# RWKV preparation in a hybrid layer: systems stored before the bonus, merged blocks evicted by ACT, new priorities

## The chip, the cores and the metric

The kernel runs on one core of a Trainium2 chip. The metric is the device time of one execution in microseconds. The core has a tensor engine (TensorE; PE in the profile, PEld for its weight loads), DVE, ACT and POOL for element-wise work, and SP, which here issues all DMAs. TensorE writes to banks of PSUM, from which DVE or ACT must copy ("evict") the results; everything else lies in SBUF, and large tensors in HBM.

## The reference, cut to what matters

One layer over 2048 tokens of width 1024. The input is modulated and projected; the projection feeds three groups of heads: (A) spatial gating, (B) RWKV-7 time mixing, (C) attention over a band of chunks. Each is gated, and one output projection with a residual and a layer norm follows. The change is in group B:

```python
def step(state, inp):
    r_t, w_t, k_t, v_t, a_t, b_t = inp
    sa = jnp.einsum('bhvk,bhk->bhv', state, a_t)
    state = state * w_t[:, :, None, :] + sa[..., None] * b_t[:, :, None, :] + v_t[..., None] * k_t[:, :, None, :]
    return state, jnp.einsum('bhvk,bhk->bhv', state, r_t)
...
y = layer_norm(y, ...)
y = y + jnp.sum(rh * kh * r_k, axis=-1, keepdims=True) * vh
```

The last line is the *bonus*: a term per token that does not need the state.

## The kernel before, in words

The tokens are cut into four stretches `u` of 512; RWKV has three pairs of heads `p`, so there are 12 RWKV *units* (p, u), counted here from 0 in the order in which they run. Within a unit there are 8 chunks of 64 tokens (`C`, `NC8`). Inside a chunk the recurrence is written as a triangular system, so that the state moves only once per chunk. A unit passes through these steps, each a Python generator:

- `rwkv_prep`: products with the small decay matrices (PE rows `rwp<-lo,lora`), scan and exponentials, then for each half of the chunks (four chunks, `c0`) the products of all keys with all queries (the Gram products, PE rows `rwp<-lr,bk` and `at<-lr,bk`). DVE evicts them with a mask: one diagonal half goes to `gb` (the systems), the other is written into `lr`. POOL scales the systems in `gb` by `rnc`. Then the 32 x 32 blocks of the systems are transposed on DVE (`gt`, in the buffers named `rc`), stored to HBM by four DMAs (`nd`), loaded back in another layout by four more (`ns`, one buffer only), and `ti` is loaded with the start of the solution. Last come the scaling of `bk` by `pend` on POOL and the bonus: `kp`, its high and low part, two products with `ones_r`, and `bon`, of which there are two buffers.
- `rwkv_solve`: 31 steps of forward substitution on DVE, two instructions each (`pr<-ti,ns` and `ti<-pr`). The solution goes to HBM (`td`) and back as `tt`. Two small groups of 16 products (PE rows `rwp<-pr,gb` and `rwp<-tt,pr`) merge the 32 x 32 blocks into 64 x 64 ones; the result of each is evicted into SBUF by two copies (`xx`, in the buffer named `pr`, and `tt`).
- `rwkv_late`: transposes and values that the chain needs.
- `rwkv_chain`: for each chunk three dependent products on TensorE with ACT and DVE work between them (PE rows `rc<-sv,lr`, `rc<-rhs,tt`, `rc<-sav,bt`), and after every fourth chunk the outputs (`rc<-sv,lr` of 64 columns and `rc<-sad,gb`). The chains of the 12 units follow each other, since the state is carried.
- `rwkv_post`: norm, four transposes (PE rows `rwp<-kc,pg`), bonus and gate, store of `y`; it frees the unit's gate buffer (`gateb`, two of them) and its `bon`.

Beside these run other generators: the projections (PE rows `pj<-hh,wh`, `pj<-hl,wh`, `pj<-hh,wl`: groups of 24 products of 512 columns; products into a tile `pj` are counted below as "projections", from the kernel's first one on), attention units (PE rows `sc`, `at<-kc,pexp`, `at<-pT,vt`), gating units (`at<-kc,tmp`), and at the end the output projection (also `pj`).

The order of all instructions is set while the kernel is built. A planner (`Model`, `drive`) keeps a clock for every engine, steps through the generators, lets a generator go on when what it yields is ready by that clock, and orders the instructions of each engine by readiness and priority. `until(key)` holds a generator back until a key is in `done`. `PREP` and `SOLVE` give each unit a priority for its preparation and for its solve. The engines then run the orders exactly as written.

In `rwkv_prep` before, everything from the transpose on waits for `("solved", previous unit)`; the unit is announced (`sent`) at the very end, after the bonus; `prepare` begins a unit when `("post", the unit two before)` is done.

Of the kernel before, what the change touches and what calls it, by code (L numbers as in the profile page):

```python
# [11 lines left out]
ALU = mybir.AluOpType  # L12
# [8 lines left out]
C = 64  # L21
NOSYNC = mybir.DependencyInfo(mybir.DependencyClass.NoSync, mybir.DependencyReason.DATA)
NC8 = U // C
# [254 lines left out]
def kernel(  # L278
# [7 lines left out]
    PE, V, A, G, SP = (Engine(md, e, n) for e, n in ((nc.tensor, "PE"), (nc.vector, "DVE"), (nc.scalar, "ACT"), (nc.gpsimd, "POOL"), (nc.sync, "SP")))  # L286
# [68 lines left out]
    mask = kc[:, K_MASK:K_MASK + 128]  # L355
# [76 lines left out]
    done = set()  # L432
# [12 lines left out]
    def until(*keys):  # L445
        while not all(k in done for k in keys):
            yield None
# [131 lines left out]
    HS = [slice(0, 64), slice(64, 128)]  # L579
    OS = [slice(64, 128), slice(0, 64)]  # L580
    c3 = lambda ap: ap.rearrange("p (c t) -> p c t", t=C)


    def rwkv_prep(p, u, before):
        yield from need(("lo", u), ("k", p, u), ("r", p, u), ("v", p, u))
        lo, k, r, v = (got[n] for n in (("lo", u), ("k", p, u), ("r", p, u), ("v", p, u)))
        b = P_PAIR + p * N_PAIR
# [18 lines left out]
        pend = sb([128, NC8], "pend", bufs=2)  # L606
# [7 lines left out]
        bk = sb([128, NC8, 2, C], "bk")  # L614
        lr = sb([128, NC8, 2, 2, C], "lr", bufs=2)
# [8 lines left out]
        for h in range(2):  # L624
            q = HS[h]
# [3 lines left out]
        for h in range(2):  # L629
            q = HS[h]  # L630
# [13 lines left out]
        rnc = sb([128, NC8], "rnc", bufs=2)  # L644
# [5 lines left out]
        gb = sb([128, NC8, 2, C], "gb", bufs=2)  # L650
        for c0 in range(0, NC8, 4):
            yield R(bk, lr, banks=("rwp", "at"))
            pg = rwp(), at()
            for c in range(4):
                for h in range(2):
                    q = HS[h]
                    mm(pg[h][:, c * 128:(c + 1) * 128].rearrange("p (s t) -> p s t", s=2), bk[q, c0 + c].rearrange("p s t -> p (s t)"),
                       lr[q, c0 + c, :, h, :])
            for h in range(2):
                for q, o in ((HS[h], gb[HS[h], c0:c0 + 4]), (OS[h], lr[OS[h], c0:c0 + 4, :, h, :])):  # L660
                    V.tensor_tensor(o, pg[h][q].rearrange("p (c s t) -> p c s t", c=4, s=2),
                                    mask[q].rearrange("p (s t) -> p s t", s=2).unsqueeze(1).to_broadcast([64, 4, 2, C]), ALU.mult)

        G.tensor_tensor(gb[:, :, 0, :], gb[:, :, 0, :], rnc.unsqueeze(2).to_broadcast([128, NC8, C]), ALU.mult)
        if before:
            yield from until(("solved",) + before)

        nd = dr([4, NC8, 32, 32], "nd", 2)
        td = dr([32, 32, 32], "td", 2)
        gt = sb([128, NC8, C], "rc", bufs=2)  # L670
        V.transpose(gt, gb[:, :, 0, :])
        for q in range(4):
            SP.dma_start(nd[q].rearrange("c t s -> t c s"), gt[32 * q:32 * q + 32, :, 32 * (q % 2):32 * (q % 2) + 32])
        ns = sb([128, 32, 32], "ns")
        for j in range(4):
            SP.dma_start(ns[32 * j:32 * j + 32].rearrange("p t s -> p (t s)"), nd.rearrange("q c t s -> (q c) (t s)"))
        V.memset(ns.rearrange("p t s -> p (t s)")[:, 0:1024:33], 1.0)
        ti = sb([128, 8, 32], "ti")
        SP.dma_start(ti.rearrange("p j i -> p (j i)"), cst[:, K_T0:K_T0 + 256])


        G.tensor_tensor(bk.rearrange("p c s t -> p c (s t)"), bk.rearrange("p c s t -> p c (s t)"),
# [8 lines left out]
        pbn = rwp()  # L691
        mm(pbn, ones_r, rkh, True, False)
        mm(pbn, ones_r, rkl, False, True)
        bon = sb([128, U], "bon", bufs=2)
        V.tensor_tensor(bon, pbn, v, ALU.mult)

        if p == 2:
            free(("lo", u))
        free(("r", p, u), ("k", p, u))
        unit[p, u] = dict(p=p, u=u, bk=bk, lr=lr, gb=gb, v=v, bon=bon, pend=pend, rnc=rnc, ns=ns, ti=ti, td=td)  # L700
        done.add(("sent", p, u))


    def rwkv_solve(s):
        p, u, gb, ns, ti, td = (s[n] for n in ("p", "u", "gb", "ns", "ti", "td"))
        yield R(ns, ti)
        pr = sb([128, 8 * 32], "pr")
        for i in range(1, 32):
            prv = pr[:, 0:8 * (i + 1)].rearrange("p (j s) -> p j s", j=8)
            V.tensor_tensor(prv, ti[:, :, 0:i + 1],  # L710
                            ns[:, i, 0:i + 1].unsqueeze(1).to_broadcast([128, 8, i + 1]), ALU.mult)
            V.tensor_reduce(ti[:, :, i], prv, AX.X, ALU.add)
            if i % 2:
                yield R(ti)
        for j in range(4):
            SP.dma_start(td.rearrange("y j i -> y (j i)")[:, j * 256:(j + 1) * 256],
                         ti[32 * j:32 * j + 32].rearrange("p j i -> p (j i)"))
        tt = tts[uorder.index((p, u)) % 2]
        for q in range(4):
            o = 32 * (q % 2)  # L720
            SP.dma_start(tt[32 * q:32 * q + 32, :, q // 2, o:o + 32],
                         td[8 * q:8 * q + 8].rearrange("c j i -> j c i"))
        tn = sb([128, NC8, 32], "pr")
        for h in range(2):
            q = slice(64 * h, 64 * h + 32)
            V.transpose(tn[q], tt[q, :, h, 0:32])
        yield R(tn, banks=("rwp",))
        px = rwp()
        for c in range(NC8):
            for h in range(2):  # L730
                a, z = 64 * h, 64 * h + 32
                mm(px[z:z + 32, c * 32:(c + 1) * 32], gb[a:a + 32, c, 0, 32:64], tn[a:a + 32, c, :])
        xx = sb([128, NC8, 32], "pr")
        for h in range(2):
            z = 64 * h + 32
            V.tensor_copy(xx[z:z + 32], px[z:z + 32, 0:256].rearrange("p (c t) -> p c t", t=32))
        yield R(xx, banks=("rwp",))
        px = rwp()
        for c in range(NC8):
            for h in range(2):  # L740
                a, z = 64 * h, 64 * h + 32
                mm(px[a:a + 32, c * 32:(c + 1) * 32], xx[z:z + 32, c, :], tt[z:z + 32, c, h, 32:64])
        for h in range(2):
            a = 64 * h
            V.tensor_copy(tt[a:a + 32, :, h, 32:64], px[a:a + 32, 0:256].rearrange("p (c t) -> p c t", t=32))
        s["tt"] = tt


# [276 lines left out]
    unit = {}  # L1025
# [246 lines left out]
    ORDER = [z.split() for z in ("B0 C0 G0 C1 B1 A0 G1 B2 C2 G2 A1", "A1 B0 C0 G0 C1 B1 G1 C2 B2 G2 A0",  # L1272
                                 "A0 C0 B0 G0 B1 C1 C2 B2 G1 G2 A1", "A1 B0 G0 B1 C0 A0 G1 B2 C1 G2 C2")]

    PREP = [4, 4, 4, 4.5, 2, 4, 4, 4, 6.5, 6.5, 5.5, 4]
    SOLVE = [4.5, 4, 3, 2, 4, 4, 6.5, 4, 3, 2, 2, 5.5]
    pprio, sprio = [4], [4]
    uorder = [(int(w[1]), u) for u in range(NU) for w in ORDER[u] if w[0] == "B"]

# [26 lines left out]
    def prepare():  # L1306
        yield from until("tables")
        for n, (p, u) in enumerate(uorder):
            if n > 1:
                yield from until(("post",) + uorder[n - 2])  # L1310
            pprio[0] = md.prio = PREP[n]
            yield from rwkv_prep(p, u, uorder[n - 1] if n else None)
            if n:
                yield from until(("chain",) + uorder[n - 1])
            yield from rwkv_late(unit[p, u])
            done.add(("late", p, u))
# [271 lines left out]
```

## Time and profile before

| what | us |
|---|---|
| median of 3 runs | 1390.93 (1387.76 to 1392.09) |
| the profiled execution, its own time | 1389.66 |
| its span | 1387.9 |
| TensorE busy | 1332.3 (96%) |
| DVE busy | 982.7 (71%) |
| ACT busy | 561.9 (40%) |
| POOL busy | 394.4 (28%) |
| mean granted TensorE clock | 0.981 |

The times are of the whole program on the device; the span runs from the first to the last instruction, and 1.8 us lie around it. A row of a timeline gives start, length, engine, operation and tiles; in brackets the idle time of the engine before it and what ended it. A row of a group gives the number of instructions, then busy us, mean ns of one, and idle time before them. In the table of stretches a row gives the stretch, its length, then for PE, PEld, DVE, ACT and POOL the busy us with the number of instructions, the mean granted clock, the DMA engines' busy share and GB/s.

### The profile page before, as it was taken

The page shows a single profiled execution, that of the slowest core. Times are in us where ns is not written, and L with a number is a line of the kernel's source. Part 1 is how long each engine was busy: PE and PEld are TensorE (multiplying, and loading weights), DVE is VectorE, ACT ScalarE, POOL GpSimd, SP SyncE. Part 2 cuts the span into 40 slices and gives each one's busy share as a digit, 9 for nine tenths or more (in the row PEclk, how much of TensorE's full clock was granted, in tenths as well). Part 3 has the DMA queues.
Part 4 walks back from the last instruction along what each step waited for, and adds up shares of the span by engine and source line. Part 5 has one row for each costly group of instructions (what it writes and reads, how often), then busy time and mean ns, then how long its engine had stood idle before and what let it go on. Part 6 is the DMA issues. An engine that isn't in the chain of part 4 may idle for free.

```text
span 1387.9 us, 23637 instructions
## 1 busy us (share of the span) xinstructions
PE 1332.3 (96%) x8698; PEld 1043.8 (75%) x8698; DVE 982.7 (71%) x2330; ACT 561.9 (40%) x1200; POOL 394.4 (28%) x433
## 2 busy tenths in 40 slices
PE   9999998999999999899999999899999999989997
PEld 8867775777777787787777777688778787768886
DVE  6676966968867668686678689866687559645665
ACT  4355435434343544532542444533323454432221
POOL 0052652344401302230323323124221130014554
PEclk9999997989999999999999999999999999999999
DMA  9566763665545264367278774354545447745663
GB/s 352 206 220 237 264 233 121 198 207 204 182 135 151 90 206 151 113 233 253 96 226 264 225 248 148 117 155 155 176 139 157 152 145 250 240 146 161 190 192 109
DMA packets 143779, 258.35 MB, mean 186 GB/s; under 512 B 37936, under 2 KB 66736, under 8 KB 143664
## 3 DMA queue, kind: packets, MB, share of 16 engines
q1 hardware_dynamic: 143664, 256.85, 56.3%
q8 instruction: 68, 1.11, 0.3%
q14 instruction: 47, 0.39, 0.1%
HBM read 188.64 MB, written 68.16 MB: 185 GB/s over the span
## 4 chain that ended last, share of the span: by engine, by line
PE 78%; DVE 8%; DMA 6%; ACT 3%; issue 2%; SPq 1%; POOL 1%; POOLq 0%; DVEq 0%; ACTq 0%
PE pj L271 53%; PE at L271 9%; PE rc L271 7%; PE rwp L271 6%; PE sc L271 5%; DMA ns<-nd 2%; DVE pr L271 1%; SPq L271 1%; DMA wl<-win 1%; DMA wr<-in_wout_dram 1%; DVE lr L271 1%; DVE ti L271 1%; DVE pexp L271 1%; DMA td<-ti 1%; DVE sv L271 1%
## 5 line engine op out<-in xcount | busy, mean ns | idle before, releaser
L271 PE MATMUL pj<-hh,wh 128*128 128x512 f32 (+1 forms) x1072 | 457.4, 427 | 0.9 <-DMA wh<-win 0.6
L271 PE MATMUL pj<-hl,wh 128*128 128x512 f32 (+1 forms) x1072 | 424.0, 396 | 1.5 <-DVE hl L271 1.5
L271 PE MATMUL pj<-hh,wl 128*128 128x512 f32 (+1 forms) x1072 | 421.7, 393 | 2.5 <-DMA wl<-win 1.9
L271 PEld LDWEIGHTS pj<-hh,wh 128*128 128x128 f32 x1072 | 203.4, 190 | 53.7 <-issue 17.6
L271 PEld LDWEIGHTS pj<-hh,wl 128*128 128x128 f32 x1072 | 202.2, 189 | 52.1 <-DMA wl<-win 4.5
L271 PEld LDWEIGHTS pj<-hl,wh 128*128 128x128 f32 x1072 | 203.5, 190 | 33.2 <-DVE hl L271 4.3
L271 POOL COPY sad<-sav 64x64 f32<-64x64 f32 x192 | 52.2, 272 | 394.1 <-ACT sav L271 388.6
L271 DVE TENSOR_TENSOR pr<-ti,ns 128x16 f32<-128x16 f32 (+30 forms) x372 | 138.3, 372 | 10.0
L271 DVE TENSOR_REDUCE ti<-pr 128x8 f32<-128x16 f32 (+30 forms) x372 | 109.9, 295 | 11.3
L271 POOL TENSOR_TENSOR wl<-wr,wh 128x1024 fp32r<-128x1024 f32 x31 | 75.1, 2422 | 130.9 <-ACT wh L271 123.1
L271 ACT ACTIVATE pexp<-pexp,nm 128x640 f32<-128x640 f32 (+4 forms) x96 | 72.7, 758 | 49.1 <-DVE nm L271 45.6
L271 DVE SCALAR_TENSOR_TENSOR sv<-sv,pend,rc 64x64 f32<-64x64 f32 x168 | 46.9, 279 | 57.7 <-PE rc L271 54.3
L271 ACT COPY pT<-at 128x512 f32<-128x512 f32 (+3 forms) x96 | 52.4, 546 | 82.7 <-PE at L271 82.0
L271 ACT ACTIVATE sav<-rc,rnc 64x64 f32<-64x64 f32 x192 | 59.0, 307 | 63.2 <-PE rc L271 60.3
L271 PE MATMUL sc<-ck_in,cq_in 64*128 64x128 f32 (+3 forms) x444 | 76.1, 398 | 2.5 <-DVE nm L271 1.7
L271 PE MATMUL at<-kc,pexp 128*128 128x128 f32 x420 | 72.4, 286 | 4.8 <-ACT pT L271 2.8
L271 DVE CUSTOM_DVE_ANT_0 pexp<-sc,bias 128x640 f32<-128x640 f32 (+4 forms) x96 | 67.5, 735 | 9.1 <-PE sc L271 5.0
L271 ACT COPY rhs<-rc 128x128 f32<-128x128 f32 x96 | 25.4, 265 | 116.2 <-PE rc L271 115.6
L271 PEld LDWEIGHTS rc<-sv,lr 128*64 128x64 f32 (+1 forms) x576 | 48.4, 161 | 29.9 <-DVE sv L271 12.4
L271 ACT CAST wh<-wr 128x1024 fp32r<-128x1024 f32 x48 | 50.1, 1045 | 47.2 <-PE pj L271 36.8
L271 PE MATMUL rc<-sv,lr 128*64 128x64 f32 (+1 forms) x576 | 57.8, 255 | 9.3 <-DVE sv L271 7.1
L271 PEld LDWEIGHTS at<-kc,pexp 128*128 128x128 f32 x420 | 49.8, 144 | 19.4 <-ACT pT L271 5.6
(326 smaller groups left out, 2285.3 us busy)
## 6 DMA issues: line engine op xcount, KB each, us to landing
wh<-win SPq DMA_DIRECT2D x82, 512.0 KB, 4.1
wl<-win SPq DMA_DIRECT2D x82, 512.0 KB, 5.0
wr<-in_win_dram SPq DMA_DIRECT2D x36, 512.0 KB, 4.8
win<-wh SPq DMA_DIRECT2D x31, 512.0 KB, 3.0
win<-wl SPq DMA_DIRECT2D x31, 512.0 KB, 3.3
wr<-y SPq DMA_DIRECT2D x24, 512.0 KB, 4.5
wo<-h SPq DMA_DIRECT2D x32, 256.0 KB, 2.5
bias<-in_btab_dram SPq DMA_DIRECT2D x24, 320.0 KB, 4.6
```

The lines of the kernel that those rows point to most:

```text
L271: r = f(*a, **k)
```

## The change

- The Gram products' two masked evictions are put in another order: first both halves of `gb`, then POOL scales these four chunks of the systems at once, then the parts that go to `lr`.
- Transpose and store (`nd`) no longer wait for the previous unit's solve; only the load `ns` does.
- The unit is announced as soon as the load is issued. Scaling of `bk` and the bonus follow. `bon` is written once the post step of the unit two before is done; `prepare` now waits for that unit's chain alone.
- The four copies that evict the merged blocks of a unit go to ACT instead of DVE.
- The two tables of priorities have other numbers.

```diff
-    def rwkv_prep(p, u, before):
+    def rwkv_prep(p, u, before, two_before):
...
             for h in range(2):
-                for q, o in ((HS[h], gb[HS[h], c0:c0 + 4]), (OS[h], lr[OS[h], c0:c0 + 4, :, h, :])):
-                    V.tensor_tensor(o, pg[h][q]..., mask[q]..., ALU.mult)
-
-        G.tensor_tensor(gb[:, :, 0, :], gb[:, :, 0, :], rnc.unsqueeze(2).to_broadcast([128, NC8, C]), ALU.mult)
-        if before:
-            yield from until(("solved",) + before)
+                q = HS[h]
+                V.tensor_tensor(gb[q, c0:c0 + 4], pg[h][q]..., mask[q]..., ALU.mult)
+            G.tensor_tensor(gb[:, c0:c0 + 4, 0, :], gb[:, c0:c0 + 4, 0, :], rnc[:, c0:c0 + 4]..., ALU.mult)
+            for h in range(2):
+                q = OS[h]
+                V.tensor_tensor(lr[q, c0:c0 + 4, :, h, :], pg[h][q]..., mask[q]..., ALU.mult)
...
         V.transpose(gt, gb[:, :, 0, :])
         for q in range(4):
             SP.dma_start(nd[q].rearrange("c t s -> t c s"), gt[...])
+        if before:
+            yield from until(("solved",) + before)
         ns = sb([128, 32, 32], "ns")
...
+        unit[p, u] = s = dict(p=p, u=u, bk=bk, lr=lr, gb=gb, v=v, pend=pend, rnc=rnc, ns=ns, ti=ti, td=td)
+        done.add(("sent", p, u))
...
+        if two_before:
+            yield from until(("post",) + two_before)
         bon = sb([128, U], "bon", bufs=2)
...
-        unit[p, u] = dict(...)
-        done.add(("sent", p, u))
+        s.update(bon=bon)
...
-            V.tensor_copy(xx[z:z + 32], px[z:z + 32, 0:256]...)
+            A.copy(xx[z:z + 32], px[z:z + 32, 0:256]...)
...
-            V.tensor_copy(tt[a:a + 32, :, h, 32:64], px[a:a + 32, 0:256]...)
+            A.copy(tt[a:a + 32, :, h, 32:64], px[a:a + 32, 0:256]...)
...
-    PREP = [4, 4, 4, 4.5, 2, 4, 4, 4, 6.5, 6.5, 5.5, 4]
-    SOLVE = [4.5, 4, 3, 2, 4, 4, 6.5, 4, 3, 2, 2, 5.5]
+    PREP = [5.5, 4, 2, 5.5, 2, 4.5, 4, 4, 6.5, 6.5, 4.5, 4]
+    SOLVE = [6.5, 4, 3, 2, 4, 4, 6.5, 4, 4, 2, 2, 3]
...
-                yield from until(("post",) + uorder[n - 2])
+                yield from until(("chain",) + uorder[n - 2])
```

Three places in the order show how instructions move. A name is followed by its buffer's number. First TensorE at the end of stretch u = 0, around the projection 504, the last of an attention gate. In the order before:

```order
L271 MATMUL pj_2119<-hh_142_578,wl_2048 128x512
L271 MATMUL rc_2106<-rhs_2155,tt_11_103 128x128
L271 MATMUL rc_2106<-sav_1243,bt_1194 128x128
L271 MATMUL at_2180<-kc_67,cv_in_2044 128x128 x4
L271 MATMUL sc_2190<-ck_in_1992,cq_in_2104 128x128 x2
L271 MATMUL rc_2106<-sv_1242,lr_758 128x128
L271 MATMUL sc_2207<-ck_in_1992,cq_in_2104 128x256 x2
L271 MATMUL rc_2106<-rhs_2202,tt_11_103 128x128
L271 MATMUL at_2222<-kc_67,pexp_2193 128x128
L271 MATMUL rc_2106<-sav_1243,bt_1194 128x128
```

The run goes on like this to 96 products (the end of unit 0's chain, an attention unit, post of unit 0) before the next projection stands. In the order after, the same two projection groups:

```order
L271 MATMUL pj_2260<-hh_142_578,wh_2144 128x512
L271 MATMUL pj_2260<-hl_143_579,wh_2144 128x512
L271 MATMUL pj_2260<-hh_142_578,wl_2143 128x512
L271 MATMUL pj_2347<-hh_105_271,wh_2254 128x512
L271 MATMUL pj_2347<-hl_106_272,wh_2254 128x512
```

Nothing stands between them; the other work of that place has moved ahead of it, between earlier projections.

Second, TensorE near the end of stretch u = 2, behind projection 1992. Before:

```order
L271 MATMUL pj_8201<-hh_1081_5769,wl_8111 128x512
L271 MATMUL sc_8322<-ck_in_8159,cq_in_7711 128x128
L271 MATMUL sc_8322<-ck_in_8159,cq_in_7711 128x384
L271 MATMUL sc_8322<-ck_in_8159,cq_in_7711 128x256
L271 MATMUL sc_8322<-ck_in_7488,cq_in_7711 128x128
L271 MATMUL sc_8322<-ck_in_7488,cq_in_7711 128x256
L271 MATMUL sc_8322<-ck_in_7488,cq_in_7711 128x128
L271 MATMUL at_8348<-kc_67,pexp_8291 128x128 x4
L271 MATMUL at_8358<-kc_67,pexp_8295 128x128 x4
L271 MATMUL rwp_8364<-kc_67,pg_7747 128x128 x4
L271 MATMUL pj_8372<-hh_1052_5636,wh_8198 128x512
```

After, the first rows of a run of 72 products that also ends with four transposes of `pg`:

```order
L271 MATMUL pj_8059<-hh_1081_5780,wl_7931 128x512
L271 MATMUL rc_8063<-sav_7247,bt_7208 128x128
L271 MATMUL at_8171<-kc_67,pexp_8098 128x128 x4
L271 MATMUL rc_8063<-sv_7246,lr_6715 128x128
L271 MATMUL at_8180<-kc_67,pexp_8098 128x128
L271 MATMUL at_8180<-kc_67,pexp_8094 128x128
L271 MATMUL rc_8063<-rhs_8178,tt_11_103 128x128
L271 MATMUL at_8187<-pT_8125,vt_7446 64x128 x2
L271 MATMUL at_8187<-pT_8125,vt_7443 64x128 x8
L271 MATMUL rc_8063<-sav_7247,bt_7208 128x128
L271 MATMUL at_8212<-kc_67,tmp_8201 128x128 x4
L271 MATMUL rc_8063<-sv_7246,lr_6715 128x128
```

More than two chunks of a chain and the post step now stand behind that projection. Other runs of products without a projection, by the same count, before and after: behind projection 1056 0 and 76; behind 1344 34 and 38; behind 2088 63 and 95; behind 705 21 and 1.

Third, SP around the solution of unit 9 (`td`, `tt`) and the system of unit 10 (`nd`, `ns`). Before:

```order
L271 DMA td_9721<-ti_9734 32x256 x4
L271 DMA tt_12_104<-td_9721 32x8x32 x4
L271 DMA wh_10395<-win_386_1722 128x1024
L271 DMA wl_10394<-win_386_1722 128x1024
L271 DMA ti_10437<-in_cst_dram 128x256
L271 DMA nd_10423<-rc_10425 32x8x32 x4
L271 DMA wh_10530<-win_392_1761 128x1024
L271 DMA wl_10529<-win_392_1761 128x1024
L271 DMA ns_10431<-nd_10423 32x1024 x4
```

After:

```order
L271 DMA nd_10190<-rc_10192 32x8x32 x4
L271 DMA wh_10313<-win_366_1626 128x1024
L271 DMA wl_10312<-win_366_1626 128x1024
L271 DMA td_9726<-ti_9739 32x256 x4
L271 DMA tt_12_104<-td_9726 32x8x32 x4
L271 DMA wh_10400<-win_382_1730 128x1024
L271 DMA wl_10399<-win_382_1730 128x1024
L271 DMA ns_10499<-nd_10190 32x1024 x4
L271 DMA ti_10505<-in_cst_dram 128x256
```

The store of unit 10's system stands ahead of unit 9's solution now, the load still behind it.

More of the change, by code (lines that the diff above doesn't have):

```diff
@@ L659, in rwkv_prep @@
             for h in range(2):
-                for q, o in ((HS[h], gb[HS[h], c0:c0 + 4]), (OS[h], lr[OS[h], c0:c0 + 4, :, h, :])):
-                    V.tensor_tensor(o, pg[h][q].rearrange("p (c s t) -> p c s t", c=4, s=2),
-                                    mask[q].rearrange("p (s t) -> p s t", s=2).unsqueeze(1).to_broadcast([64, 4, 2, C]), ALU.mult)
-        G.tensor_tensor(gb[:, :, 0, :], gb[:, :, 0, :], rnc.unsqueeze(2).to_broadcast([128, NC8, C]), ALU.mult)
-        if before:
-            yield from until(("solved",) + before)
+                q = HS[h]
+                V.tensor_tensor(gb[q, c0:c0 + 4], pg[h][q].rearrange("p (c s t) -> p c s t", c=4, s=2),
+                                mask[q].rearrange("p (s t) -> p s t", s=2).unsqueeze(1).to_broadcast([64, 4, 2, C]), ALU.mult)
+            G.tensor_tensor(gb[:, c0:c0 + 4, 0, :], gb[:, c0:c0 + 4, 0, :], rnc[:, c0:c0 + 4].unsqueeze(2).to_broadcast([128, 4, C]), ALU.mult)
+            for h in range(2):
+                q = OS[h]
+                V.tensor_tensor(lr[q, c0:c0 + 4, :, h, :], pg[h][q].rearrange("p (c s t) -> p c s t", c=4, s=2),
+                                mask[q].rearrange("p (s t) -> p s t", s=2).unsqueeze(1).to_broadcast([64, 4, 2, C]), ALU.mult)
         nd = dr([4, NC8, 32, 32], "nd", 2)
@@ L699, in rwkv_prep @@
         free(("r", p, u), ("k", p, u))
-        unit[p, u] = dict(p=p, u=u, bk=bk, lr=lr, gb=gb, v=v, bon=bon, pend=pend, rnc=rnc, ns=ns, ti=ti, td=td)
-        done.add(("sent", p, u))
+        s.update(bon=bon)
     def rwkv_solve(s):
@@ L735, in rwkv_solve @@
             z = 64 * h + 32
-            V.tensor_copy(xx[z:z + 32], px[z:z + 32, 0:256].rearrange("p (c t) -> p c t", t=32))
+            A.copy(xx[z:z + 32], px[z:z + 32, 0:256].rearrange("p (c t) -> p c t", t=32))
         yield R(xx, banks=("rwp",))
@@ L744, in rwkv_solve @@
             a = 64 * h
-            V.tensor_copy(tt[a:a + 32, :, h, 32:64], px[a:a + 32, 0:256].rearrange("p (c t) -> p c t", t=32))
+            A.copy(tt[a:a + 32, :, h, 32:64], px[a:a + 32, 0:256].rearrange("p (c t) -> p c t", t=32))
         s["tt"] = tt
@@ L1309, in prepare @@
             if n > 1:
-                yield from until(("post",) + uorder[n - 2])
+                yield from until(("chain",) + uorder[n - 2])
             pprio[0] = md.prio = PREP[n]
-            yield from rwkv_prep(p, u, uorder[n - 1] if n else None)
+            yield from rwkv_prep(p, u, uorder[n - 1] if n else None, uorder[n - 2] if n > 1 else None)
             if n:
```

## The prediction

> **What bounds the kernel now.** I read the page first (busy shares, granted clock, the chain that ended last), then the stretches of time in which TensorE ran no projection.
>
> ```profile
> PE 1332.3 (96%) x8698; PEld 1043.8 (75%) x8698; DVE 982.7 (71%) x2330; ACT 561.9 (40%) x1200; POOL 394.4 (28%) x433
> ...
> PEclk9999997989999999999999999999999999999999
> ...
> PE 78%; DVE 8%; DMA 6%; ACT 3%; issue 2%; SPq 1%; POOL 1%; POOLq 0%; DVEq 0%; ACTq 0%
> ```
>
> TensorE is busy for 96% of the span and carries 78% of the chain that ended last. The change adds and removes no product, so it can move the time only where TensorE stands idle, runs at a halved clock, or switches between kinds of product. Next the table of stretches: first seven places with little or no projection work, last the end stage, with nothing but output products.
>
> ```profile
> 215.80:244.40 28.60, 21.80 (x150) 14.81 (x149) 22.84 (x81) 17.16 (x45) 5.46 (x9) 0.72 0.26 88
> 312.50:316.80 4.30, 2.47 (x43) 1.93 (x42) 3.81 (x8) 0.75 (x2) 2.35 (x2) 1.00 0.50 203
> 571.30:583.80 12.50, 8.44 (x63) 6.44 (x63) 9.71 (x20) 5.29 (x13) 1.99 (x5) 0.73 0.46 146
> 820.60:825.60 5.00, 3.71 (x54) 2.79 (x53) 3.08 (x7) 1.54 (x4) 1.27 (x1) 1.00 0.89 310
> 829.10:833.90 4.80, 3.44 (x24) 2.48 (x25) 4.60 (x11) 4.46 (x12) 0.00 (x0) 1.00 0.67 218
> 872.60:890.10 17.50, 13.02 (x107) 9.29 (x106) 15.46 (x53) 10.52 (x26) 1.75 (x6) 0.90 0.37 126
> 1234.10:1242.00 7.90, 2.09 (x31) 1.47 (x29) 2.83 (x7) 2.66 (x5) 2.10 (x3) 0.81 1.03 292
> 1260.00:1370.00 110.00, 110.00 (x476) 88.92 (x475) 70.03 (x126) 25.55 (x32) 55.77 (x38) 1.00 0.56 178
> ```
>
> The last row is the yardstick: 476 products of 512 columns in 110 us, 0.231 us each, no idle time. In the other rows "busy" is too kind, since a matmul's duration includes waiting in the pipeline. So I gave each record the spacing to the next start that this pair of forms shows elsewhere at full clock (the 30th percentile over the trace). By that the 148 records of the first hole are worth 8.3 us of its 28.6. The excess over work is 20.2 us there, then 2.6, 9.6, 2.6, 2.4, 12.3 and 6.5 us: 56 us in seven places. Of the other runs of non-projection products, those of a single kind (181 of 389) have no excess at all.
>
> In the order before, each hole has one reason: the planner has no projection that it may issue, because a buffer of the evacuated result is not free (the first hole waits for the gate buffer that the post step of RWKV unit 0 releases), so TensorE is left with dependent steps of one chain and attention tile.
>
> **The change part by part.** The span is 1387.9 us, the profiled execution took 1389.66 us, 1.3 us under the median of 1390.93. The sum is made on 1389.66.
>
> *Merged blocks on ACT.*
>
> ```profile
> L271 DVE COPY pr<-rwp 32x256 f32<-32x256 f32 x24 | 10.2, 423 | 2.0 <-PE rwp L271 1.5
> ...
> L271 DVE COPY tt<-rwp 32x256 f32<-32x256 f32 x24 | 10.0, 415 | 3.5 <-PE rwp L271 3.3
> ...
> L271 ACT COPY pg<-rc 128x256 f32<-128x256 f32 x24 | 8.9, 372 | 39.5 <-PE rc L271 33.3 <-DVE pr L271 6.0
> ```
>
> 48 copies leave DVE (20.2 us) and go to ACT. ACT's price for 256 elements from PSUM is the third row, 0.37 us, so 17.9 us more on an engine at 40%. On the path each merge has two pairs of copies in a row; 0.05 us less each, against ACT's queue, where one instruction ahead can cost up to 1 us. Bounds -2 to +5 us over 12 units; I take 0, because the two waits shown for the DVE copies come to 4.8 us in all and their place on TensorE is between other products.
>
> *Systems scaled by halves, stored first.*
>
> ```profile
> 767.44 1.05 POOL L271 TENSOR_TENSOR gb<-gb,rnc 128x512 f32<-128x512 f32 x1
> ...
> 776.46 0.70 DVE L271 STREAM_TRANSPOSE rc<-gb 128x512 f32<-128x512 f32 x1
> ...
> 786.22 2.09 SPq L271 DMA_DIRECT2D ns<-nd  x4
> ```
>
> These are three steps of unit 7. Scaling on POOL becomes 24 instructions of half the length; a half costs between 0.52 us (half of 1.05) and 1.05, so 0 to 12.6 us more on POOL, 28% busy, off the path. The first half now runs while DVE masks. The transpose came 8 us after the scaling, because it stood behind the wait for the previous solve; then four stores on SP, then the load. After the change only the load waits. I found this wait ahead of the transpose in 4 units of 12 (2, 3, 7, 10); elsewhere the store is not delayed, and the gain there is nothing. Where it is, the 9.8 us between transpose and load leave the path of that unit's solve. On SP nothing new stands behind a waiting instruction: the stores wait for the transpose alone, and the loads stood behind the same wait before.
>
> *Unit announced before the bonus; the bonus waits for post n-2; preparation waits for chain n-2 only.*
>
> ```profile
> 790.15 0.69 DVE L271 TENSOR_TENSOR bon<-rwp,bv_in 128x512 f32<-128x512 f32 x1
> ...
> 794.36 0.18 DVE L271 TENSOR_TENSOR pr<-ti,ns 128x16 f32<-128x16 f32 x1
> ```
>
> In unit 7 the bonus was over 3.5 us before the solve could begin; the load of the system held it, not the announcement, so I cost it at 0. In unit 11 the bonus did end after the load, but that unit's chain ends behind projection 3024 in both orders, so it is 0 there too. Preparation may start earlier by the length of the post step, which the end of the trace shows bare:
>
> ```profile
> 1236.97 0.61 PE L271 MATMUL rc<-sad,gb 128*64 128x128 f32 x8
> 1241.99 1.22 PE L271 MATMUL pj<-bk,wh 128*128 128x512 f32 x2 [4.41 <-ACT wh L271]
> 1243.25 0.79 PE L271 MATMUL pj<-bk,wl 128*128 128x512 f32 x1
> 1243.85 1.12 PE L271 MATMUL rwp<-kc,pg 128*128 128x128 f32 x4
> ```
>
> From the chain's last product to the transposes of post: 6.9 us. That is up to 6.9 us per unit, used only where r, k, v are there.
>
> *Priorities, and so the order.* What these parts are worth is decided by where holes stand now. The chain's own latency is read in the hole at 872:
>
> ```profile
> 874.56 0.49 PE L271 MATMUL rc<-sav,bt 128*128 128x128 f32 x2 [0.73 <-ACT sav L271]
> ...
> 885.78 1.07 PE L271 MATMUL rc<-sad,gb 128*64 128x128 f32 x8
> ```
>
> Two whole chunks and the output: 11.2 us, with some attention between. Counting projections in both orders as a clock that stands still in a hole:
>
> 1. First hole (after projection 504): gone, since unit 0's chain ends before it. -20.2.
> 2. 312 us: its run of 21 products is broken up. -2.0.
> 3. New run of 76 products at projection 1056 (gate buffer, post of unit 3): the last chunk's half, by the rows above 4.1 us, then 6.9 to post, then one attention product group of about 1.5: 12.5 us with 4.9 of work, +7.6; the neighbours at 957 shrink by 3.4 (from 5.6 to 2.2, by their number of kinds). +4.2.
> 4. 571 us: one chunk less in it (3.3 us). -3.3.
> 5. 820 and 829 us: one run of 72 products now, with exactly the chain steps of the 11.2 us, then 6.9 to post and 0.4: 18.5 us with 6.4 of work, 12.1, where 5.0 was. +7.1.
> 6. 872 us: 95 products instead of 63, with three attention tiles and one chain step instead of two tiles and three chunks. Between 14 and 22 us of length with 5.9 of work; I take 18, the row's 17.5 being nearest. 0 (-4 to +4).
> 7. The end: TensorE stood 4.41 us for the split of the first output tile, whose load is issued behind the last gating unit. By the order that load comes about 10 projections and one chain step earlier (3 us). -3.0.
> 8. [...] +1.7.
> 9. Switches from projections to others and back: 396 before, 410 now. One costs what these rows show, 0.32 to the next start instead of 0.23.
>
> ```profile
> 1230.85 0.48 PE L271 MATMUL pj<-hh,wh 128*128 128x512 f32 x1
> 1231.17 0.40 PE L271 MATMUL pj<-hl,wh 128*128 128x512 f32 x1
> 1231.40 0.40 PE L271 MATMUL pj<-hh,wl 128*128 128x512 f32 x1
> ```
>
> 14 x 0.09: +1.3.
> 10. Unit 0's merge is asked for some 17 us earlier (projection 327 instead of 387) while its Gram products stand 3.5 us later. Faster solve (23 other DVE instructions in it, not 31) and table sent back without other DMAs between can give that, but barely; late by 0 to 10 us, I take +2.
>
> Sum: -20.2 - 2.0 + 4.2 - 3.3 + 7.1 + 0 - 3.0 + 1.7 + 1.3 + 2.0 = -12.2 us; 1377.5 on the profiled scale, **1378 us** beside the median.
>
> [...]
>
> **The rivals.**
>
> *The hole only moves (about the same time).* RWKV units follow each other; what the first hole gave, runs 3, 5 and 6 take back as chain steps that now wait there. For it: the new runs hold the same dependent steps. Against it: terms 3 and 5 together are 11.3, not 20.2. It needs run 6 at its upper bound (+4) and the merge of unit 0 late by 7: 1387 to 1395 us.
>
> *Unit 7's solve comes too late (slower).* Its 62 solving instructions ran from 794.36 to this row:
>
> ```profile
> 839.24 0.43 DVE L271 TENSOR_TENSOR pr<-ti,ns 128x256 f32<-128x256 f32 x1
> ```
>
> 45.3 us, with 20 us of other DVE work between by the order. In the order after 91 other instructions stand between, 46 us at their mean durations: some 71 us. Its merge stands inside run 6, where nothing else can go on, while the end of solve 6 also moved back. If the earlier store does not win those 25 us, TensorE waits there. It decides above 12 us of lateness; with the whole 25 us the time is 1403.
>
> *More than forecast.* Run 6 without the chain is short (14 us, -4), ACT evicts at once, unit 0 is on time (-2), the end loses all of its 4.4: 1366 to 1370.
>
> **How the numbers follow.** Forecast 0.53 (1371 to 1386), the hole moves 0.18, the late solve 0.13 (1396 to 1405), more than forecast 0.16. The range 1366 to 1395 leaves out the late solve and a little below: about 0.83 inside. A change under 0.3% (4.2 us) can't be told from none, so faster means under 1386.8 and slower over 1395.1: faster is forecast, the better case and a little of the moved hole, 0.71; same 0.16; slower 0.13.
>
> **What would show it.** In the profile after: slices seven and eight of the page near full clock; no stretch near 210 to 240 us without projections; a stretch of 11 to 16 us around projection 1056 (420 to 455 us) and one of 16 to 21 us some 800 to 830 us in; DVE near 963 us, ACT near 580. A TensorE wait of more than 3 us on the copies or transposes ahead of unit 0's merge makes term 10 too small; one over 12 us inside the 95-product run makes the slower rival right; if the first hole stays, the forecast falls as a whole.

## The result, and the profile after

| what | before | changed |
|---|---|---|
| median of 9 runs, us | 1388.72 (1384.95 to 1392.09) | 1397.01 (1395.08 to 1403.71) |
| ratio, 95% interval | | 1.0066 (1.0047 to 1.0086) |
| profiled execution / span, us | 1389.66 / 1387.9 | 1403.12 / 1401.3 |
| mean granted TensorE clock | 0.981 | 0.973 |

The change makes the kernel 0.7% slower; 1378 was forecast, 19 us too low. The profiled execution of the changed kernel is 6 us above its median, so lengths from it are partly too long; where that matters, the same stretch is shown from other executions too.

From the page of the changed kernel: busy shares, granted clock, the chain that ended last.

```profile
PE 1337.9 (95%) x8698; PEld 1050.0 (75%) x8698; DVE 953.6 (68%) x2282; ACT 579.2 (41%) x1248; POOL 396.0 (28%) x445
...
PEclk9999999899998999999999999799999999999999
...
PE 72%; DVE 11%; DMA 8%; ACT 3%; issue 3%; POOL 2%; SPq 1%; POOLq 0%; DVEq 0%; ACTq 0%
```

DVE has lost the copies and ACT has them (the prediction named 963 and 580 us). But TensorE's share of the last chain fell from 78 to 72%, DVE and DMA gained, and TensorE's idle time (span less busy) grew from 55.6 to 63.4 us: TensorE waits more. The clock's dips now stand in other slices. The table of stretches of the changed kernel: the new stretch behind projection 240; the place of the old first hole; the runs behind 1056, 1992 and 2088; the run ahead of the output products; the end stage.

```profile
129.70:140.70 11.00, 5.03 (x25) 2.41 (x25) 10.35 (x34) 3.78 (x6) 2.44 (x2) 0.75 0.47 171
215.80:244.40 28.60, 28.60 (x172) 21.19 (x172) 21.95 (x61) 16.62 (x33) 12.98 (x8) 1.00 0.70 249
436.80:453.80 17.00, 11.64 (x139) 8.68 (x137) 8.11 (x20) 7.64 (x18) 2.16 (x4) 0.76 0.27 71
818.70:836.50 17.80, 11.96 (x112) 8.86 (x110) 14.83 (x40) 9.59 (x24) 5.85 (x11) 0.95 0.81 281
878.90:902.00 23.10, 17.38 (x165) 12.90 (x162) 11.71 (x33) 10.82 (x23) 0.00 (x0) 0.66 0.42 126
1251.80:1256.90 5.10, 3.29 (x32) 2.38 (x30) 3.44 (x6) 1.93 (x4) 0.47 (x2) 0.79 1.12 337
1275.00:1385.00 110.00, 110.00 (x476) 88.94 (x475) 69.89 (x127) 25.43 (x32) 57.39 (x40) 1.00 0.56 178
```

The first hole is gone: its 28.6 us now hold 172 products at full clock. The end stage is as before. In place of the hole stand four stretches, three forecast and one not, and a fifth that is not in the table: the runs behind projections 600 and 603, from 263.6 to 277.7 us, where TensorE waits for an ACT copy.

```profile
267.88 1.63 PE L271 MATMUL at<-pT,vt 128*64 128x128 f32 x16 [3.94 <-ACT pT L271]
```

Below, the "excess" of a run is measured as in the prediction: elapsed time less the spacings that the same pairs of products have elsewhere. It depends somewhat on which pairs serve as the measure, so read it to about 1 us.

The profiled executions differ by 13.4 us of span: 7.8 us are idle time of TensorE, 5.6 us are busy time of the same 8698 products, which a lower clock lengthens (19.2 us at a clock of 0.82 and 23.2 at 0.63 for the same 165 products, the rows of x1 and x6 below). By an estimate from mean clock and span, what the granted clock can have cost at most is (1 - 0.981) x 1387.9 = 26.4 us before and (1 - 0.973) x 1401.3 = 37.8 after. These two executions exaggerate the difference: the same figure is 28.8 us on average over the executions of the kernel before whose clock is on record (0.974 to 0.985), and 32.4 us over the nine of the changed kernel (0.973 to 0.980), so 3.6 us more.

With the projections as a clock: the changed kernel is 11.5 us ahead behind the old first hole, 12.3 ahead at projection 1056 and 4.7 behind after the run that stands there, 3.2 ahead at 1657, 11.7 behind after the run behind 2088 and 13.4 behind at the end (profiled executions). All that the first hole gave is spent by the run behind 1056; some comes back at 1344, and the loss proper falls between 1657 and 2089.

### The profile page after: what moved, and what is told of

It reads as the page before. It is cut to its first block, busy times and chain, and to the rows that moved or that the text cites. A ratio compares the mean times of both kernels' runs of the same rounds, so it can differ in the third digit from the quotient of the medians.

```text
span 1401.3 us, 23672 instructions
## 1 busy us (share of the span) xinstructions
PE 1337.9 (95%) x8698; PEld 1050.0 (75%) x8698; DVE 953.6 (68%) x2282; ACT 579.2 (41%) x1248; POOL 396.0 (28%) x445
## 4 chain that ended last, share of the span: by engine, by line
PE 72%; DVE 11%; DMA 8%; ACT 3%; issue 3%; POOL 2%; SPq 1%; POOLq 0%; DVEq 0%; ACTq 0%
PE pj L271 48%; PE at L271 8%; PE rc L271 6%; PE rwp L271 5%; PE sc L271 4%; DVE pr L271 2%; DMA wl<-win 2%; DVE ti L271 2%; DMA wr<-in_wout_dram 1%; SPq L271 1%; DMA h<-in_xt_dram 1%; DMA td<-ti 1%; DMA tt<-td 1%; DVE pexp L271 1%; ACT hh L271 1%
## 5 line engine op out<-in xcount | busy, mean ns | idle before, releaser
L271 ACT ACTIVATE pexp<-pexp,nm 128x640 f32<-128x640 f32 (+4 forms) x96 | 72.7, 758 | 50.1 <-DVE nm L271 46.1
L271 DVE CUSTOM_DVE_ANT_0 pexp<-sc,bias 128x640 f32<-128x640 f32 (+4 forms) x96 | 68.2, 735 | 12.2 <-PE at L271 7.3
L271 ACT COPY rhs<-rc 128x128 f32<-128x128 f32 x96 | 25.5, 266 | 117.7 <-PE rc L271 117.3
L271 PE MATMUL at<-pT,vt 128*64 128x128 f32 x840 | 60.3, 291 | 6.2 <-ACT pT L271 3.9
```

The lines of the kernel that those rows point to most:

```text
L271: r = f(*a, **k)
```

## Experiments

Unless said otherwise each was timed in three rounds beside the kernel before; ratios are to that kernel, with 95% intervals. The changed kernel has 1.0066 (1.0047 to 1.0086).

### The parts of the change, each alone and in pairs

Three parts were set or unset: the tables, the copies (DVE or ACT), and the code of `rwkv_prep` and `prepare` (store first, early announcement, later bonus: "store").

```diff
 tables  -    PREP = [4, 4, 4, 4.5, 2, 4, 4, 4, 6.5, 6.5, 5.5, 4]
         +    PREP = [5.5, 4, 2, 5.5, 2, 4.5, 4, 4, 6.5, 6.5, 4.5, 4]      (SOLVE likewise)
 copies  -    V.tensor_copy(xx[z:z + 32], px[z:z + 32, 0:256]...)
         +    A.copy(xx[z:z + 32], px[z:z + 32, 0:256]...)                 (tt likewise)
 store   the rest of the diff of the change
```

> The kernel before with nothing changed but the two tables of priorities. If the lost time comes from where the tables put the work (theory 'place'), this order has the same runs at projections 1056 (97 products; 76 in the changed kernel) and 2088 (95 products, the same three attention tiles) as the changed kernel, and a rest of the first hole (46 products at projection 504, some 14 us instead of 28.6): excess some 9 + 12 + 9 + 17 us in the four runs against 45 in the kernel before; 1385 to 1398 us, with the half-clock stretch behind run 2088 that the changed kernel shows. If the lost time comes from the edits of the code (theory 'edits'), the tables alone keep what the first hole gave, 1372 to 1383 us.

> The changed kernel with the two tables of the kernel before: all edits of the code, no new priorities. By 'place': the first hole is back and longer (119 products with five chunks of a chain, some 35 us), one of 106 products stands at 1992 (four chunks and a post, some 23 us), run 2088 is short (42 products, 12 us): 1395 to 1408 us, for a reason that has nothing to do with the edits' own costs. By 'edits' (copies on ACT, store first, early announcement cost or save something at each unit): the same offset as between the changed kernel and the tables alone, in each of the 12 units alike, about 0.7 us a unit.

> The changed kernel with the four copies of the merged blocks on DVE again. If ACT's queue makes the merges late (a rival to 'place'; waits of 1.6 and 0.2 us on these copies in the trace of the changed kernel), it is 5 to 10 us faster than the changed kernel, 1387 to 1392 us. By 'place' the copies are worth under 2 us and the time is set by the new places: runs of 48 products at 1056 (11 us), 106 at 1992 (23 us), 57 at 2055, 65 with four chunks at 2088 (18 us): 1395 to 1408 us.

> The kernel before with the systems' order, the early store, the early announcement and the later bonus, but copies on DVE and the old tables. By 'place': first hole of 120 products (35 us), 79 at 1992 (18 us), 83 with three chunks at 2088 (20 us): 1395 to 1408 us. If the early store and announcement by themselves are worth something, the solves begin earlier in every unit and the time is under the kernel before's, 1375 to 1385 us.

> The kernel before with nothing changed but the four copies on ACT (old tables). By 'place' the planner's new order decides: runs of 58 products at 504 (two chunks and a post, 18 us instead of 28.6), 46 at 1344 (14 us), 75 at 1992 (two chunks and a post, 17 us), 74 at 2088 (three chunks and three attention tiles, 22 us), 50 at 2943 (5 us): excess 12 + 11 + 11 + 16 + 3 against 45 in the kernel before, so 1395 to 1405 us. If copies on ACT are worth something by themselves, 1380 to 1388 us.

> The kernel before with the copies on ACT and the new tables; store, announcement and bonus as before. Runs of 53 products at 1053 (10 us), 80 at 1992 (four chunks and a post, 23 us), 112 at 2088 (four chunks and a post, 30 us), no first hole: excess 5 + 17 + 22 against 45 in the kernel before, 1388 to 1398 us by 'place'. If the store and announcement are what costs, it is at 1383 to 1390 us.

| run | tables | copies | store | median us | ratio |
|---|---|---|---|---|---|
| t1_tables_alone | new | DVE | old | 1391.75 | 1.000 (0.9975 to 1.0025) |
| t5_copies_alone | old | ACT | old | 1411.84 | 1.0174 (1.0136 to 1.0213) |
| t6_copies_and_tables | new | ACT | old | 1414.77 | 1.0187 (1.0168 to 1.0205) |
| t4_store_and_announce_alone | old | DVE | new | 1407.81 | 1.0116 (1.0082 to 1.015) |
| t2_edits_alone | old | ACT | new | 1417.72 | 1.0185 (1.0151 to 1.0219) |
| t3_copies_on_dve | new | DVE | new | 1411.26 | 1.0141 (1.0102 to 1.0181) |

No part gains alone, and the effects don't add: copies on ACT cost 1.7% on the kernel before (t5) and gain 0.75% (1.0141 to 1.0066) with the new tables and the new store code. So no part has a price of its own that could be read off here; each re-sorts the whole order, and what is timed is the order. t1 is the plainest case: its first hole has shrunk from 20.2 to some 6 us of excess, and the time is the same; in its trace 9.0 us appear at 1056, some 5.5 at 2304 and 17 instead of 12.3 at 2088. By the lengths of the runs I expected t2, t3, t5 and t6 some 10, 3, 7 and 17 us or more too fast; the direction of "place" held, its sizes did not. Every part run with an edit of the code is slower than the kernel before, so these runs leave open that the edits cost something by themselves; the section on taking the runs away comes back to it.

### The stretch behind projection 240: where a wait goes when it is taken away

TensorE in the changed kernel:

```profile
130.77 1.12 PE L271 MATMUL rwp<-lo,lora 64*128 64x512 f32 x2
137.08 2.07 PE L271 MATMUL at<-lo,lora 64*128 64x512 f32 x2 [5.20 <-DVE gate L271]
```

Unit 1's second decay product waits for bank `at`, which a DVE instruction of an attention unit empties. What DVE and POOL do meanwhile:

```profile
123.81 2.37 POOL L271 TENSOR_TENSOR wl<-wr,wh 128x1024 fp32r<-128x1024 f32 x1 [5.36 <-ACT wh L271]
124.11 2.11 DVE L271 TENSOR_TENSOR pr<-ti,ns 128x16 f32<-128x16 f32 x1
126.25 0.17 DVE L271 TENSOR_REDUCE ti<-pr 128x8 f32<-128x16 f32 x1
126.45 0.18 DVE L271 TENSOR_TENSOR pr<-ti,ns 128x24 f32<-128x24 f32 x1
...
131.55 2.38 POOL L271 TENSOR_TENSOR wl<-wr,wh 128x1024 fp32r<-128x1024 f32 x1 [5.37 <-ACT wh L271]
132.05 2.00 DVE L271 TENSOR_TENSOR pr<-ti,ns 128x96 f32<-128x96 f32 x1
...
136.75 0.28 DVE L271 SCALAR_TENSOR_TENSOR gate<-at,gate 128x128 f32<-128x128 f32 x1
```

Unit 0's solve, whose priority the tables raise from 4.5 to 6.5, stands ahead of the gate. Two of its steps take 2.11 and 2.00 us where the steps after them take 0.18 and 0.26: they end, at 126.22 and 134.05 us, when POOL's `wl<-wr,wh` ends (126.18 and 133.93).

The tables alone don't make this wait. In t1 and t6 (new tables, old store code) the gate stands at 128.5 and 127.9 us on DVE, the decay products come at 137.4 and 136.8 us, and they wait for nothing. Only t3, which has tables and store code together, waits as the changed kernel does (5.18 us at 136.7). Together the two put the decay products 6 us earlier on TensorE and the gate 8 us later on DVE.

Three runs change places on the engines and nothing else.

```diff
+        for e, i, j in [("DVE", 178, 163)]:                     # x1: the gate above, 15 places up
+            self.order[e].insert(j, self.order[e].pop(i))
 x5:     [("DVE", 178, 163), ("DVE", 194, 171)]                  # and the next gate product, 23 up
 x2:     x1's, and ("ACT", 221, 210), ("ACT", 225, 224), ("ACT", 226, 225),
         ("SP", 276, 274), ("SP", 277, 275), ("SP", 278, 276),
         ("ACT", 770, 766), ("ACT", 771, 767), ("ACT", 772, 768)
```

> The changed kernel with one DVE instruction moved 15 places up on DVE, all else in the same order: the attention gate that empties bank at for unit 1's second decay product stands ahead of 12 solving steps of unit 0 instead of behind them. In the trace of the changed kernel TensorE waits 5.20 us for it at 131 us. If such waits add up (theory 'the order is followed to the letter, so each late instruction is paid in full'), 4 to 6 us faster than the changed kernel: 1391 to 1393 us. If TensorE only comes earlier to the next hole (rival 'the next wait takes it'), under 2 us: 1395 to 1397 us.

> The changed kernel with two DVE instructions moved: the attention gate of x1_gate_first, and the gate product of the same tile (512 columns), which in x1_gate_first made TensorE wait 5.47 us 15 projections later, 23 places up, both ahead of unit 0's solving steps. If unit 0's solve, which the new tables put in front, is what holds TensorE there, the 7 us that x1_gate_first gained at projection 240 are now kept past 255: 5 to 7 us faster than the changed kernel, 1389 to 1392 us. If a third wait takes them (everything on DVE behind the solve is late alike), under 2 us: 1395 to 1397 us.

> The same with four more moves at the places where TensorE's longest waits stand in the changed kernel: ACT's copy of pT ahead of the next stretch's inputs (3.94 us at 264), the last three loads of unit 3's solution ahead of two loads of weights on SP (3.17 us at 442), ACT's two exponentials ahead of a load-bound input at 880 (2.14 us), ACT's copies of unit 1's merged blocks ahead of an input that waits for its load (1.59 us at 273). Together with the first 16 us. If the waits are paid in full, 12 to 16 us faster than the changed kernel: 1381 to 1385 us, below the kernel before. If the next wait takes them, under 6 us: 1391 us or more.

Measured: x1 1396.92 us, 1.0057 (1.0038 to 1.0077); x5 1397.56, 1.0049 (1.0029 to 1.007); x2 1397.51, 1.0057 (1.0037 to 1.0077). None can be told from the changed kernel. The traces show why. In x1 the wait is gone and projection 240 starts 7 us earlier; TensorE in x1, 15 projections later, and in x5, 33 later:

```profile
143.03 1.11 PE L273 MATMUL at<-kc,cv_in 128*128 128x128 f32 x4 [5.47 <-DVE gate L273]
```

```profile
148.73 1.22 PE L273 MATMUL sc<-ck_in,cq_in 64*128 64x256 f32 x4 [5.32 <-DVE nm L273]
```

Each time the next attention instruction behind the solve takes the same 5 us back, and projection 288 starts 0.4 us earlier in x1 and 0.8 in x5. So the debt is not that instruction's: with the solve in front, DVE's attention work behind it is late too. x2 shows the same at 264 us, where ACT's earlier copy of `pT` only brought TensorE sooner to unit 1's merge:

```profile
268.32 0.31 PE L273 MATMUL rwp<-pr,gb 32*32 32x32 f32 x2 [4.56 <-DVE pr L273]
```

I had expected the waits to be paid in full; of the places moved in x2 only the loads on SP kept their gain in its trace (the run behind 1056 is 5.6 us shorter than in the changed kernel), and x2's time does not show it: its run behind 2088 is longer (25.5 us instead of 23.1).

### The one wait that counts: loads split on SP

SP, DVE and TensorE at unit 3's merge, which stands inside the run behind 1056 in the changed kernel:

```profile
437.73 0.33 SPq L271 DMA_DIRECT2D tt<-td  x1
438.15 0.40 SPq L271 DMA_DIRECT2D wh<-win  x1
438.65 0.38 SPq L271 DMA_DIRECT2D wl<-win  x1
439.08 1.45 SPq L271 DMA_DIRECT2D tt<-td  x3
...
444.63 0.44 DVE L271 STREAM_TRANSPOSE pr<-tt 32x256 f32<-32x256 f32 x1 [4.36 <-DMA tt<-td]
...
445.12 0.69 PE L271 MATMUL rwp<-pr,gb 32*32 32x32 f32 x30 [3.17 <-DVE pr L271]
```

Two loads of weights (512 KB each) stand between the four small loads of the solution; the last lands over 4 us after it is issued. x6 has x5's two moves and the SP part of x2:

```diff
+        for e, i, j in [("DVE", 178, 163), ("DVE", 194, 171), ("SP", 276, 274), ("SP", 277, 275), ("SP", 278, 276)]:
+            self.order[e].insert(j, self.order[e].pop(i))
```

> The same two moves, and unit 3's loads of the solution ahead of two loads of weights on SP; in x2_five_moves that move kept 5.6 us at projection 1056. If both places are independent, 10 to 13 us faster than the changed kernel: 1384 to 1387 us, under the kernel before. If the run behind 2088 takes part of it back, as in x2_five_moves (25.5 us there instead of 23.1), 1388 to 1394 us.

1392.42 us, 1.0023 (1.0008 to 1.0038): clear of the changed kernel's interval, and 5 us under x5, whose interval it overlaps by 0.0009. The gain is half of the 10 us and more that two independent gains would have given. The same place in x6:

```profile
433.08 1.81 SPq L273 DMA_DIRECT2D tt<-td  x4
434.99 0.40 SPq L273 DMA_DIRECT2D wh<-win  x1
...
436.06 0.43 DVE L273 STREAM_TRANSPOSE pr<-tt 32x256 f32<-32x256 f32 x1
...
437.64 0.69 PE L273 MATMUL rwp<-pr,gb 32*32 32x32 f32 x32
```

The merge goes through without a wait; the run takes 12.96 us instead of 17.03, and x6 stays ahead of x5 to the end. Since x2 has the same three moves on SP and no better time, the price of 5 us rests on the pair x5 and x6.

### The run behind 2088 and the clock

```diff
+        n = int(gap / 0.3)          # gap: TensorE's planned wait, for waits in this run alone
+        for k in range(n):
+            in_order(nc.tensor.matmul(t[:, 0:128], ones_r, ones_r, start=True, stop=True).ins)
```

> The changed kernel with 16 products of 128 columns that nobody reads, put into four waits of the run behind projection 2088 and nowhere else; order otherwise unchanged. The changed kernel runs at half clock from 897 to 914 us, 12 us of it projections. If idle windows in this run set the clock, the half-clock stretch shrinks or goes: 4 to 8 us faster than the changed kernel, 1389 to 1393 us. If 1.8 us of products spread over 23 us are too little to hold the clock, they only cost their own time: 0 to 2 us slower, 1397 to 1399 us.

16 products that nobody reads stand in the waits of this run. 1399.93 us, 1.008 (1.006 to 1.0101): no gain. In the changed kernel's trace the clock is 0.50 from 886.2 to 903.1 us, of which all but the last 1.1 us lie inside the run, and 1.00 from 903.2 to 914; the 897 to 914 us of the expectation were wrong. The trace of x3 tells less than I hoped, since the same run without the 16 products varies as much. The row of this stretch in x1 and in x6 (in the changed kernel it is the fifth row of the table above):

```profile
877.90:897.10 19.20, 13.88 (x165) 10.00 (x164) 11.30 (x32) 10.80 (x23) 0.00 (x0) 0.82 0.51 152
```

```profile
869.90:893.10 23.20, 17.88 (x165) 13.30 (x164) 11.55 (x33) 10.57 (x23) 0.00 (x0) 0.63 0.42 124
```

The same 165 products take 19.2 us (x1) at a clock of 0.82 and 23.2 (x6) at 0.63 (x5 23.3 at 0.63, x2 25.5 at 0.67, x3, with its 16 more, 20.4 at 0.83). TensorE's idle time in the two rows is the same, 5.32 us; the 4.00 us are busy time. How the clock falls inside a run of dependent products is worth 4 us, and what decides it in an execution stays open.

### Taking the runs away

The projections' generator waits for the buffer of its result before its first product. In x4 only the evacuation waits:

```diff
-            while not room(tag, bufs):
-                yield None
-            take(tag, key)
...
             if not left:
+                tag, bufs = items[i][0][2:]
+                while not room(tag, bufs):
+                    yield None
+                take(tag, key)
                 got[key] = evac(pts[i])
```

u1 adds tables found by a search over the planner's own end; u2 and u3 are the kernel before with this rule, u2 with searched tables of its own; u4 is u2 with the stores and loads of the solutions at priority 7.

```diff
 u1  +    PREP = [5.5, 3, 2.0, 5.5, 4.5, 3, 5.5, 4.0, 6.5, 4.5, 3, 4.5]
     +    SOLVE = [6.5, 4.0, 3.0, 2, 4, 4.0, 2, 4, 4.5, 4, 4.5, 3.0]
 u2  +    PREP = [2, 4, 3, 2, 2, 4.0, 4, 3, 3, 5.5, 5.5, 4]
     +    SOLVE = [4.5, 4.5, 6.5, 4.5, 4.0, 5.5, 4, 4.0, 4, 4, 4.5, 2]
 u4  +    pr0, md.prio = md.prio, 7      (ahead of the store td; put back behind the loads tt)
```

> The changed kernel with projections allowed to start before the buffer for their result is free; only the evacuation waits. If the runs of products without a projection are held by those buffers alone, 24 projections (5.5 us) can go into each of the runs at 504, 1056, 1344, 1992 and 2088, which have 12, 4, 12 and 17 us of excess (504 none): 10 to 20 us faster than the changed kernel, 1377 to 1387 us. If the waiting work is only moved behind the next group, where it stands without cover again, no more than 3 us: 1394 to 1400 us.

> The changed kernel with projections allowed to start before the buffer for their result is free (as x4_buffer_later) and other tables, so that its order has no run of more than 52 products without a projection (longest: 52 at 957, 46 with two chunks at 2112, 35 at three places; the changed kernel has 76, 72 and 95). If the long runs are the cause, the 12 + 12 + 17 us of excess there shrink to some 2 + 9, and the half-clock time from 77 us to some 30: 25 to 35 us faster than the changed kernel, 1362 to 1372 us. If the changed code costs by itself (copies, store, announcement), or if the waits only spread over more places, 1380 us or more.

> The kernel before with the same later buffer and tables of its own; longest runs 57 at 528 with one chunk and a post, 43 with two chunks at 2112, 42 at 939 and 2568. If the runs are the cause and the code of the change is worth nothing either way, within 5 us of u1_changed_code_no_runs: 1362 to 1375 us. If the code of the change costs 5 to 9 us by itself, it is that much faster than u1_changed_code_no_runs.

> The kernel before with the later buffer alone and its old tables: runs of 57 at 528 (one chunk and a post), 98 with two chunks and a post at 888, 52 and 40 with a post at 1269 and 1272, 46 with a post at 2016, 52 at 2112. The first hole (20.2 us of excess) turns into some 8 + 12 us at two places: no change within 0.4%, 1385 to 1394 us, if the length of runs decides. If the rule by itself covers 5.5 us in each run, 1370 to 1380 us.

> u2_code_before_no_runs with the store and the loads of every solution at a higher priority, so that on SP no load of weights stands between them. In x6_gates_and_loads the same for one unit was worth 5 us. If such a split costs at other units too, 3 to 8 us faster than u2_code_before_no_runs; if it cost only because unit 3's merge stood inside a run, no change within 3 us.

The last two columns are of the profiled execution; the kernel before has 55.6 us and 0.981 there, the changed one 63.4 us and 0.973.

| run | median us | ratio | TensorE idle, us | mean clock |
|---|---|---|---|---|
| x4_buffer_later | 1392.80 | 1.0022 (1.0002 to 1.0041) | 62.4 | 0.987 |
| u3_before_buffer_later | 1395.23 | 1.0037 (1.0018 to 1.0055) | 63.9 | 0.980 |
| u1_changed_code_no_runs | 1368.86 | 0.9844 (0.9827 to 0.986) | 49.6 | 0.995 |
| u2_code_before_no_runs | 1367.16 | 0.9832 (0.9816 to 0.9849) | 47.9 | 0.989 |
| u4_loads_first | 1366.50 | 0.9819 (0.9805 to 0.9834) | 46.1 | 0.989 |

The rule alone does little on either code: x4 gained 4 us on the changed kernel instead of the 10 to 20 expected, since a run of 93 products with four chunks now stands behind 2112 (22 us long). With searched tables, whose orders have no run of more than 57 products, both codes are 1.6 to 1.7% faster than the kernel before, and within each other's intervals. So with orders chosen alike the changed code costs nothing that can be measured. That the length of the runs is what these orders save is the likely reading and not a separate proof: the search chose by the planner's whole time, so its tables may have removed short waits too. From u1's page:

```profile
PE 1315.4 (96%) x8698; PEld 1031.5 (76%) x8698; DVE 950.7 (70%) x2282; ACT 579.2 (42%) x1248; POOL 400.1 (29%) x445
...
PEclk9999999999999999999999999999999999999999
```

The same 8698 products as in the changed kernel, with 22.5 us less of busy time, 13.8 us less of idle time, and no slice with a clock under 0.9. u4's higher priority for the loads is no different from u2, although it does what it should: in u2 loads of weights split the solution's loads at units 8 and 10, in u4 nowhere. So a split costs only at some places; that those are merges inside a run fits x6 and is not shown further. The kernels u1, u2 and u4 beat both the kernel before and the changed one.

## Why the prediction was wrong

**Right.** Terms 1, 2, 5 and 7: the first hole is gone whole (20.2); the 312 us run is broken up; the run behind 1992 has 11.7 us of excess (12.1 forecast); the end is 2.7 us shorter (3.0). Term 4 was better than forecast (9.6 to 3.8, so 5.8 instead of 3.3).

**Term 10 failed, by what it asked.** It asked whether unit 0's merge would be late on TensorE and took +2. The merge was in time, because the solve had been put in front on DVE; what was late was DVE's attention work behind it. The stretch behind 240 has 9.8 us of excess, and x1 and x5 show that moving one or two late instructions does not win it back. The order after showed the solve's place on DVE; the prediction counted the instructions in the solve (23) and not those that the solve now holds up.

**A place without a term.** The runs behind 600 and 603 have some 10 us of excess between them, where the run with the same merge (unit 1's) had some 3 before. TensorE waits there 3.94 us for ACT's copy of `pT` and 1.59 us for ACT's copy of the merged block. The sum has nothing for this place; the first part of the change was put at 0 for all merges together. t3, with these copies on DVE, has the 4 us wait for `pT` too, so the copies are not its cause.

**Term 3 was mis-sized:** excess 12.2 instead of 7.6. Of the difference 3.17 us is the wait for the split loads of `tt`. On SP the prediction looked at what stands behind waiting instructions, not at large loads between four small ones that TensorE needs within the run; x6 shows that this place is worth some 5 us.

**Term 6 was mis-sized:** 23.1 us instead of 18, excess 17.3 against 12.3 before, so +5.0 where 0 (-4 to +4) stood. The bounds came from a row at a clock of 0.90; three attention tiles, each waiting for its predecessor, run at 0.63 to 0.83. By all executions of the same products (19.2 to 25.5 us against 17.5 before) it is +2 to +8.

**Term 8 looked for the clock in the wrong place:** +1.7 for projections behind the holes. No run shows this term: in the changed kernel the clock stayed at 0.50 for 4.6, 2.0, 5.1 and 1.1 us behind the runs at 240, 1056, 1992 and 2088. Much of the half-clock time lies inside the runs (0.75, 0.76 and 0.66 in the table of stretches), where it lengthens dependent products (23.2 us in x6 at 0.63, 19.2 in x1 at 0.82), so part of it is already in terms 3 and 6 and in the stretch at 240. By the estimate from clock and span the clock can have cost 11.4 us more in the profiled executions (37.8 against 26.4); on average over the executions it is 3.6 us more. So 1.7 is some 2 us short of that estimate for a usual execution, and terms 10, 3 and 6 with the place that has no term carry most of the miss.

**The rivals.** "The hole only moves" names in the main what happened: runs at 240, 600, 1056 and 2088 took back what the first hole gave, and more; 1397 lies 2 us above its range. Its condition on unit 0's merge did not hold. t1 shows the moved hole without the code of the change, at 1.000. "Unit 7's solve comes too late" had the right time for a wrong reason. The solve did grow past the 71 us forecast: DVE's first and last step, and TensorE's merge, in the changed kernel:

```profile
798.45 0.17 DVE L271 TENSOR_TENSOR pr<-ti,ns 128x16 f32<-128x16 f32 x1
...
884.24 0.41 DVE L271 TENSOR_REDUCE ti<-pr 128x8 f32<-128x256 f32 x1
```

```profile
890.71 1.06 PE L271 MATMUL rwp<-pr,gb 32*32 32x32 f32 x32
```

86 us; yet the merge row has no bracket, TensorE came from an attention product straight to it. The waits inside the run are for attention tiles (2.14 us for `nm`, three of about 0.7 us for ACT's copies of `pT`).

**Beneath the terms** lies one assumption: that the excess of a hole that goes is gained in full, and that new runs cost their latency at the clock of the old ones. That assumption failed: in t1, x1, x2 and x5 a place that was freed let TensorE come sooner to work that was not ready.

## What to carry to other kernels

Where an engine's order is fixed and followed to the letter, price an edit by the longest runs of dependent work that its order leaves bare, and read each at the clock that such a run is granted (0.63 to 0.83 behind 2088), not at full speed. Taking away one wait gained nothing where the engine waited for was itself behind (x1 1396.92 us, x5 1397.56, the changed kernel 1397.01): look at what it does next, here 15 and 33 projections on. Here each edit of the code alone lost the order that had been tuned for the code before (1.2% in t4, 1.7% in t5), so compare edits only when each has an order of its own: the later buffer and the searched tables moved 1.6%, the edits nothing that could be measured (u1 against u2).

## What the runs showed of the hardware

- Two DVE instructions that take 0.17 and 0.26 us elsewhere in the changed kernel (the same shapes, 0.17 at 798.45 and 0.26 at 914.81) took 2.11 and 2.00 us while POOL subtracted two SBUF tensors, and ended with it to within 0.12 us (rows at 124.11 and 132.05). POOL's two instructions took 2.37 and 2.38 us. What holds DVE there was not shown.
- The same 165 products of one run took 19.2 us in x1 and 23.2 in x6, at granted clocks of 0.82 and 0.63, though TensorE's work and order there were identical. TensorE's idle time was 5.32 us in both; the profile shows the clock as the difference, not its cause.
- Four loads that are issued together landed in time for unit 3's merge (x6: issued from 433.08 us on, DVE's transpose at 436.06, no wait on TensorE); with two loads of 512 KB issued between them the last made TensorE wait 3.17 us (the changed kernel).
